# FOX's running sums of the forget gates spread to all partitions by a DMA through DRAM, in a two-layer block of four mixers on one NeuronCore

## Chip, cores and metric

One NeuronCore of a Trainium2 chip runs the whole program in one launch. The metric is the device time of one execution in microseconds (us), lower is better. All tensors are fp32. The large products split both operands into a high and a low fp32r part and add three products (high by high, high by low, low by high).

## What is computed

Two layers over 512 tokens of width 1024. Each layer has a mixer with four branches (FOX, dilated attention, retention, MLA), gates, an output projection and a feed-forward part. The change concerns FOX, a causal softmax attention with four heads of width 64 whose scores get a decay: for each head the running sum over the tokens of the log of a forget gate.

```python
log_f = jax.nn.log_sigmoid((ff + b_forget).astype(jnp.float32))
decay = jnp.cumsum(log_f, axis=1).transpose(0, 2, 1)
o_a = causal_block_attention(heads(fq, FOX_HEADS), heads(fk, FOX_HEADS), heads(fv, FOX_HEADS),
                             HEAD_DIM ** -0.5, decay)
...
s = jnp.einsum('bhqd,bhkd->bhqk', qi, k).astype(jnp.float32) * scale
s = s + args[2][..., :, None] - decay[..., None, :]
s = jnp.where(kpos[None, :] <= qpos[:, None], s, -jnp.inf)
p = jax.nn.softmax(s, axis=-1).astype(v.dtype)
return jnp.einsum('bhqk,bhkd->bhqd', p, v)
```

The decay enters twice: of the query's token (one value per partition, since queries lie on the partitions) and of the key's token (one value per column, the same in all partitions). The second is what has to be spread.

## The kernel before

**The large products and their weights.** Activations lie with features on the partitions. The projections and the gates run through `fm` (line 997 ff.): for one tile of 128 output features, 8 k-tiles of three products each, 24 weight products of 128 x 512 (`mm3`: L529, L530, L531) into a PSUM bank `acc`. Weights stream from DRAM: SP loads a block of up to 512 KB into one of three `raw` buffers (L258), ScalarE casts it to the high part `whi` (L289), VectorE subtracts for the low part `wlo` (L290). Conversions run two blocks ahead of the block in use; a `raw` buffer is free for the next load when both its conversions are done.

**The background work.** While these products run, the attention branches are slipped in between. `collect` (end of the class) counts weight products; for every 6.5 of them (`SPACING`) it calls `step()`, which first carries out what the step before deferred (`defer`, `flush`) and then advances the first generator in a queue to its next `yield`. The queue holds, in this order: MLA's preparation, MLA, dilated attention, `forget` (the running sums), FOX, retention. Here no order is written out by hand for the engines: where each instruction stands on its engine is settled when the program is built. Each engine then takes its instructions strictly in that order, SP its DMAs too.

**The running sums.** `forget` makes the log of the gates, `nl`, as 128 x 16: partition is the token within a block of 128, column 4t + h is block t of head h. `running_sum` makes the sums of the blocks before and adds two products, with the triangle `tri` (L989) and with `ones` (L990), into one PSUM bank. VectorE copies the result to `cum`, 128 x 16 (L992).

**FOX's attention** (`attention` with `kind == FOX`). There are 16 items, head h and query block i of 128 tokens; item x needs the keys of blocks 0 to i, up to 512 columns. The items are pipelined over steps: scores of x (L672, two products into a bank `b`), then the exponent of x - 1 (L681 on VectorE adds the bias and takes the row's maximum, L683 on ScalarE makes the exponential and its row sum), the normalising of x - 2 (L690 reciprocal on VectorE, L691 on GpSimd), the transposes of x - 4 (L698 on TensorE, into a bank `b`), the split of x - 5 (L708, L709), and after the last block of a head the product with the values (L752). There are four banks `b`. Before the scores are used, `make_bias` (L660, VectorE) has to make the item's bias from the mask, the query's decay (a column of `cum`) and the key's decay `dk[h]`, a tile of 128 x 512 with the same row in every partition.

`dk[h]` is made by `spread` (lines 645 to 651): four products per head, a column of `cum` repeated 128 times against the identity (L648), into a bank `b`, and a copy by ScalarE (L651). Head 0 is spread in the first step, head h + 1 after the scores of block 1 of head h, two steps ahead of its first use.

**Around it on SP.** The key tiles of FOX are rearranged by six moves of 64 partitions from SBUF to SBUF (L1099, named L1108 in the changed file) just when FOX begins; the tables of retention are loaded later by L774.

Of the kernel before, what the change touches and what calls it, by code (L numbers as in the profile page):

```python
# [9 lines left out]
F32 = mybir.dt.float32  # L10
# [197 lines left out]
class Builder:  # L208
# [425 lines left out]
    def attention(self, kind, qk, vt, out):  # L634


        nc = self.nc
        items = [(h, i) for h in range(4) for i in range(4)]
        st = {}
        dk, pts = {}, {}  # L640
        pair = {}
        mask = self.con("dil" if kind == DIL else "causal")
        cum = self.cum if kind == FOX else None

        def spread(h):
            ps = self.ps("b")
            for t in range(4):
                nc.tensor.matmul(ps[:, 128 * t:128 * t + 128], cum[:, 4 * t + h:4 * t + h + 1].to_broadcast([128, 128]),  # L648
                                 self.con("ident"), start=True, stop=True)
            dk[h] = self.a()  # L650
            self.defer(lambda: nc.scalar.copy(dk[h], ps))  # L651

        n = len(items)
        biases = {}

        def make_bias(x):
            h, i = items[x]
            L = 128 * (i + 1)
            b = self.a()
            nc.vector.scalar_tensor_tensor(b[:, :L], dk[h][:, :L], cum[:, 4 * i + h:4 * i + h + 1],  # L660
                                           mask[:, 128 * (3 - i):512], op0=ALU.subtract, op1=ALU.add)
            biases[x] = b[:, :L]
            if i == 3:
                dk.pop(h)

        def scores(x):
            h, i = items[x]
            L = 128 * (i + 1)
            qs = slice(128 * i, 128 * i + 128)
            ps = self.ps("b")  # L670
            for j, (q, k) in enumerate(qk[h]):
                nc.tensor.matmul(ps[:, :L], q[:, qs], k[:, :L], start=j == 0, stop=j == len(qk[h]) - 1)  # L672
            st[x] = ps

        def exps(x):
            i = items[x][1]
            L = 128 * (i + 1)
            ps = st.pop(x)
            A, nm, rs = self.a(), self.small(1), self.small(1)
            bias = biases.pop(x) if kind == FOX else mask[:, 128 * (3 - i):512]  # L680
            nc.vector.tensor_tensor_reduce(out=A[:, :L], in0=ps[:, :L], in1=bias, scale=-1.0, scalar=3.0e38,  # L681
                                           op0=ALU.add, op1=ALU.min, accum_out=nm)
            nc.scalar.activation(A[:, :L], A[:, :L], AF.Exp, bias=nm, scale=-1.0, accum_out=rs)  # L683
            st[x] = A, rs

        def normalise(x):
            A, rs = st[x]
            L = 128 * (items[x][1] + 1)
            rr = self.small(1)
            nc.vector.reciprocal(rr, rs)  # L690
            nc.gpsimd.tensor_scalar(A[:, :L], A[:, :L], rr, 1.0, op0=ALU.mult, op1=ALU.mult)  # L691

        def transposes(x):
            i = items[x][1]
            A = st.pop(x)[0]
            tp = self.ps("b")
            for j in range(i + 1):
                nc.tensor.transpose(tp[:, 128 * j:128 * j + 128], A[:, 128 * j:128 * j + 128], self.con("ident"))  # L698
            st[x] = tp

        def parts(x):
            h, i = items[x]
            if i == 0:
                pts[h] = (self.ptp.tile([128, 1664], F32R, tag="pth", name="pth"),
                          self.ptp.tile([128, 1664], F32R, tag="ptl", name="ptl"))
            src = st.pop(x)[:, :128 * (i + 1)].rearrange("p (j c) -> p j c", c=128)
            hi, lo = (self.pt_blocks(t, i) for t in pts[h])
            nc.scalar.copy(hi, src)  # L708
            nc.vector.tensor_sub(lo, src, hi.bitcast(F32))  # L709

        def result(h, po):
            self.pv_sum(h, po, pair)
            if h % 2 == 1:
                out[h // 2] = self.split(pair.pop(h // 2), lo_engine=nc.gpsimd)

        def at(x, f, *args):
            if 0 <= x < n:
                f(x, *args)

        if kind == FOX:  # L720
            spread(0)
            yield
            make_bias(0)
        for x in range(n + LG + 2):

            at(x - 1, exps)
            at(x - 2, normalise)
            at(x - LG - 1, parts)
            if kind == FOX:
                at(x + 1, make_bias)  # L730

            at(x, scores)
            at(x - LG, transposes)
            if 0 <= x - LG - 2 < n and items[x - LG - 2][1] == 3:
                h = items[x - LG - 2][0]
                po = self.pv(h, pts.pop(h), vt)
                self.defer(lambda h=h, po=po: result(h, po))
            if kind == FOX and x < n and items[x][1] == 1 and items[x][0] < 3:
                spread(items[x][0] + 1)
            yield  # L740
# [241 lines left out]
    def running_sum(self, nl):  # L982
        nc = self.nc
        before = self.small(16)
        nc.vector.memset(before[:, 0:4], 0.0)
        for t in range(3):
            nc.vector.tensor_add(before[:, 4 * t + 4:4 * t + 8], before[:, 4 * t:4 * t + 4], nl[:, 4 * t:4 * t + 4])
        ps = self.ps("b")
        nc.tensor.matmul(ps[:, 0:16], self.con("tri"), nl, start=True, stop=False)  # L989
        nc.tensor.matmul(ps[:, 0:16], self.con("ones"), before, start=False, stop=True)  # L990
        self.cum = self.cp.tile([128, 16], F32, tag="cum", name="cum")
        self.defer(lambda: nc.vector.tensor_copy(self.cum, ps[:, 0:16]))  # L992
        yield
        yield

# [1018 lines left out]
```

## Time and profile before

| | |
|---|---|
| median of 3 runs | 1676.44 us (1675.61 to 1676.55) |
| profiled execution, its own time | 1679.01 us |
| its span | 1677.2 us |
| TensorE clock over the span | 0.997 of full speed |
| TensorE busy (matmuls) | 1649.3 us, 98% of the span |
| VectorE / ScalarE / GpSimd busy | 1130.8 us (67%) / 851.0 us (51%) / 358.7 us (21%) |
| FOX's spread, L648 | 64 records of 275 ns at the median, 180.9 to 1043.9 us |

Times in the rows count from the span's start. PE is TensorE's products, DVE VectorE, ACT ScalarE, POOL GpSimd, SP the engine that issues most DMAs; SPq is its sequencer. The records of TensorE's products overlap, as they are pipelined, so what a product costs is read from the start of one to the start of the next and not from its length. A product of fp32 operands (not fp32r) is recorded as two passes, so the eight records of one spread are its four products. What stands in brackets behind a row is the idle time of the engine just before it, and what ended it.

### The profile page before, as it was taken

The page shows a single profiled execution, that of the slowest core. Times are in us where ns is not written, and L with a number is a line of the kernel's source. Part 1 is how long each engine was busy: PE and PEld are TensorE (multiplying, and loading weights), DVE is VectorE, ACT ScalarE, POOL GpSimd, SP SyncE. Part 2 cuts the span into 40 slices and gives each one's busy share as a digit, 9 for nine tenths or more (in the row PEclk, how much of TensorE's full clock was granted, in tenths as well). Part 3 has the DMA queues.
Part 4 walks back from the last instruction along what each step waited for, and adds up shares of the span by engine and source line. Part 5 has one row for each costly group of instructions (what it writes and reads, how often), then busy time and mean ns, then how long its engine had stood idle before and what let it go on. Part 6 is the DMA issues. An engine that isn't in the chain of part 4 may idle for free.

```text
span 1677.2 us, 26506 instructions
## 1 busy us (share of the span) xinstructions
PE 1649.3 (98%) x9746; PEld 1463.0 (87%) x9746; DVE 1130.8 (67%) x2165; ACT 851.0 (51%) x1682; POOL 358.7 (21%) x400
## 2 busy tenths in 40 slices
PE   8999999999999999999989999999999999999997
PEld 7898888788899999988878988888888989999876
DVE  6657676556469777762286576766565687777897
ACT  6666554323456555553265665533234565555665
POOL 0244333432130000000122343333321300000000
PEclk9999999999999999999999999999999999999999
DMA  5644225667735777443245452256665247775572
GB/s 205 173 107 139 82 82 175 170 169 182 213 87 144 189 186 184 95 154 99 76 148 160 108 145 76 90 175 168 173 161 178 75 137 191 186 183 153 189 234 92
DMA packets 93698, 248.88 MB, mean 148 GB/s; under 512 B 11521, under 2 KB 23041, under 8 KB 93569
## 3 DMA queue, kind: packets, MB, share of 16 engines
q1 hardware_dynamic: 72768, 205.24, 39.0%
q0 software_dynamic: 20800, 41.95, 13.6%
q8 instruction: 77, 1.26, 0.3%
q14 instruction: 53, 0.43, 0.1%
HBM read 220.93 MB, written 31.46 MB: 150 GB/s over the span
## 4 chain that ended last, share of the span: by engine, by line
PE 89%; DVE 6%; issue 2%; ACT 1%; DMA 1%; POOL 1%; DVEq 0%; SPq 0%; POOLq 0%
PE acc L529 15%; PE acc L530 15%; PE acc L531 15%; PE b L503 4%; PE b L505 4%; PE b L504 4%; PE acc L505 3%; PE acc L504 3%; PE acc L503 3%; PE b L752 2%; PE b L672 2%; PE b L698 1%; PE acc L1891 1%; PE acc L1893 1%; PE acc L1892 1%
## 5 line engine op out<-in xcount | busy, mean ns | idle before, releaser
L529 PE MATMUL acc<-a,whi 128*128 128x512 f32 (+1 forms) x1254 | 485.5, 387 | 0.0
L531 PE MATMUL acc<-a,wlo 128*128 128x512 f32 (+1 forms) x1254 | 475.2, 379 | 0.0
L530 PE MATMUL acc<-a,whi 128*128 128x512 f32 (+1 forms) x1227 | 465.3, 379 | 0.0
L289 ACT CAST whi<-raw 128x512 fp32r<-128x512 f32 (+3 forms) x398 | 214.0, 576 | 346.5 <-PE acc L530 174.7
L290 DVE TENSOR_TENSOR wlo<-raw,whi 128x512 fp32r<-128x512 f32 (+3 forms) x398 | 271.9, 713 | 133.4 <-ACT whi L289 132.7
L531 PEld LDWEIGHTS acc<-a,wlo 128*128 128x128 f32 x1254 | 236.3, 188 | 44.7
L529 PEld LDWEIGHTS acc<-a,whi 128*128 128x128 f32 x1254 | 237.1, 189 | 40.0 <-issue 1.0
L530 PEld LDWEIGHTS acc<-a,whi 128*128 128x128 f32 x1227 | 231.9, 189 | 38.9 <-issue 1.0
L405 DVE TENSOR_TENSOR wlo<-raw,whi 128x1024 fp32r<-128x1024 f32 x132 | 157.8, 1195 | 69.0 <-ACT whi L404 67.3
L404 ACT CAST whi<-raw 128x1024 fp32r<-128x1024 f32 x132 | 135.4, 1027 | 126.6 <-PE b L504 48.0
L503 PE MATMUL b<-a,whi 128*128 128x256 f32 x560 | 158.7, 283 | 0.0
L504 PE MATMUL b<-a,whi 128*128 128x256 f32 x560 | 158.5, 283 | 0.0
L505 PE MATMUL b<-a,wlo 128*128 128x256 f32 x560 | 158.5, 283 | 0.0
L1302 DVE TENSOR_TENSOR a<-acc,a 128x512 f32<-128x512 f32 x64 | 44.1, 689 | 140.0 <-PE acc L531 140.0
L503 PE MATMUL acc<-a,whi 128*128 128x256 f32 x448 | 126.8, 283 | 0.0
L504 PE MATMUL acc<-a,whi 128*128 128x256 f32 x448 | 126.8, 283 | 0.0
L505 PE MATMUL acc<-a,wlo 128*128 128x256 f32 x448 | 126.8, 283 | 0.0
L503 PEld LDWEIGHTS b<-a,whi 128*128 128x128 f32 x560 | 107.5, 192 | 0.2
L504 PEld LDWEIGHTS b<-a,whi 128*128 128x128 f32 x560 | 107.5, 192 | 0.0
L505 PEld LDWEIGHTS b<-a,wlo 128*128 128x128 f32 x560 | 107.5, 192 | 0.0
L333 POOL DMA_DIRECT2D raw<-wts x36 | 32.3, 896 | 345.8 <-DMA raw<-wts 140.6
L521 ACT CAST a<-a 128x512 fp32r<-128x512 f32 (+1 forms) x143 | 76.6, 567 | 51.8 <-DVE a L1094 10.7
(282 smaller groups left out, 3203.6 us busy)
## 6 DMA issues: line engine op xcount, KB each, us to landing
raw<-wts SPq DMA_DIRECT2D x257, 512.0 KB, 3.9
raw<-wts POOLq DMA_DIRECT2D x36, 512.0 KB, 6.9
a<-a SPq DMA_DIRECT2D x120, 128.0 KB, 2.3
sums<-wts POOLq DMA_DIRECT2D x30, 512.0 KB, 6.6
raw<-sums SPq DMA_DIRECT2D x20, 512.0 KB, 4.1
raw<-wts SPq DMA_DIRECT2D x35, 256.0 KB, 2.9
sums<-sums POOLq DMA_DIRECT2D x10, 512.0 KB, 3.7
a<-xT SPq DMA_DIRECT2D x16, 256.0 KB, 6.0
```

The source lines that it names most:

```text
L289: todo.append(lambda hi=hi, src=src, n=n: nc.scalar.copy(hi[:, :n], src))
L290: todo.append(lambda hi=hi, lo=lo, src=src, n=n: (lo_engine or nc.vector).tensor_sub(lo[:, :n], src, hi[:, :n].bitcast(F32)))
L404: self.nc.scalar.copy(hi, src)
L405: self.nc.vector.tensor_sub(lo, src, hi.bitcast(F32))
L503: mm(o, hi[:, c], x[k][0], start=first, stop=False, skip_group_check=i in (2, 3, 4, 6))
L504: mm(o, hi[:, c], x[k][1], start=False, stop=False, skip_group_check=i in (2, 3, 4, 6))
L505: mm(o, lo[:, c], x[k][0], start=False, stop=k == 3, skip_group_check=i in (2, 3, 4, 6))
L521: nc.scalar.copy(hi, src)
L529: mm(out, w[0], x[0], start=start, stop=False)
L530: mm(out, w[0], x[1], start=False, stop=False)
L531: mm(out, w[1], x[0], start=False, stop=stop)
L1302: nc.vector.tensor_mul(z, ps, self.rB)
```

## The change

The running sums are made a second time, transposed: two more products with the operands exchanged give 16 x 128, row 4t + h is block t of head h. In the step that copied `cum`, ScalarE now also copies these rows to an SBUF tile and SP writes them to a tile in DRAM, 8 KB. `spread(h)` issues one DMA on SP that reads head h's four rows of 128 and writes them to all 128 partitions. The spread's four products and ScalarE's copy are gone. One `yield` is added in the running sums and one in FOX's attention after the first spread, so FOX's scores and retention come two steps later.

```diff
         def spread(h):
-            ps = self.ps("b")
-            for t in range(4):
-                nc.tensor.matmul(ps[:, 128 * t:128 * t + 128], cum[:, 4 * t + h:4 * t + h + 1].to_broadcast([128, 128]),
-                                 self.con("ident"), start=True, stop=True)
             dk[h] = self.a()
-            self.defer(lambda: nc.scalar.copy(dk[h], ps))
+            rows = self.cum_rows.rearrange("(t h) c -> h t c", h=4)[h:h + 1]
+            nc.sync.dma_start(dk[h].rearrange("p (t c) -> p t c", t=4), rows.to_broadcast([128, 4, 128]))
...
         if kind == FOX:
             spread(0)
+            yield
             yield
             make_bias(0)
...
         self.cum = self.cp.tile([128, 16], F32, tag="cum", name="cum")
-        self.defer(lambda: nc.vector.tensor_copy(self.cum, ps[:, 0:16]))
+        rows = self.ps("b")
+        nc.tensor.matmul(rows[0:16, 0:128], nl, self.con("tri"), start=True, stop=False)
+        nc.tensor.matmul(rows[0:16, 0:128], before, self.con("ones"), start=False, stop=True)
+        self.cum_rows = self.dram.tile([16, 128], F32, tag="cum", name="cum")
+
+        def out():
+            nc.vector.tensor_copy(self.cum, ps[:, 0:16])
+            t = self.a()
+            nc.scalar.copy(t[0:16, 0:128], rows[0:16, 0:128])
+            nc.sync.dma_start(self.cum_rows, t[0:16, 0:128])
+        self.defer(out)
+        yield
         yield
         yield
```

In the changed file the lines behind `spread` have lower numbers up to the running sums (L660 becomes L657, L681 L678, L690 L687, L698 L695) and higher ones from there on (L1099 becomes L1108).

SP, where FOX begins in the first layer, with what each DMA waits for (DVE, PE, Pool, Activation: that engine; DMAHW and a number: an earlier DMA). Before, from the third last move of the keys on:

```order
L1099 DMA a<-a 64x512 [waits DMAHW7_49]
L1099 DMA a<-a 64x512 [waits DMAHW5_49,DMAHW4_49,DMAHW0_49]
L1099 DMA a<-a 64x512 [waits DMAHW7_49,DMAHW6_49,DMAHW1_49]
L258 DMA raw<-wts 128x512 [waits DMAHW2_49,DVE_49]
L258 DMA raw<-wts 128x1024 [waits DMAHW3_49,DVE_49]
L258 DMA raw<-wts 128x1024 [waits DVE_49,Activation_49]
```

And in the changed kernel:

```order
L1108 DMA a<-a 64x512 [waits DMAHW7_49]
L1108 DMA a<-a 64x512 [waits DMAHW5_49,DMAHW4_49,DMAHW0_49]
L999 DMA cum<-a 16x128 [waits DMAHW1_49,Activation_49]
L1108 DMA a<-a 64x512 [waits DMAHW7_49,DMAHW6_49,DMAHW2_49]
L258 DMA raw<-wts 128x512 [waits DMAHW3_49,DVE_49]
L648 DMA a<-cum 128x4x128 [waits DMAHW1_49]
L648 DMA a<-cum 128x4x128 [waits DVE_49]
L258 DMA raw<-wts 128x1024 [waits DVE_49]
L648 DMA a<-cum 128x4x128 [waits DMAHW4_49,PE_49,Pool_49]
L258 DMA raw<-wts 128x1024 [waits DMAHW0_49,DVE_49,Activation_49]
L648 DMA a<-cum 128x4x128 [waits DVE_49,Pool_49]
```

The write to DRAM (L999) stands between the last two moves, the first broadcast (L648) waits for it, the second for VectorE (the sum of the first exponent), the third for TensorE (the transposes of block 2), and weight loads stand between them.

VectorE at the same place, from the copy of `cum` on (`ISA` with an `a` is the exponent's sum L681, with `sm` alone its second half). Before:

```order
L992 COPY cum<-b 128x16
L764 TENSOR_TENSOR a<-b,a 64x512
L1283 TENSOR_TENSOR a<-acc,a 128x512
L290 TENSOR_TENSOR wlo<-raw,whi 128x256 x2
L1285 SCALAR_TENSOR_TENSOR a<-a 128x512
L660 SCALAR_TENSOR_TENSOR a<-a,cum,ct 128x128
L660 SCALAR_TENSOR_TENSOR a<-a,cum,ct 128x256
L681 ISA a,sm_2326<-b,a 128x128
L681 ISA sm_2326 128x1
L660 SCALAR_TENSOR_TENSOR a<-a,cum,ct 128x384
L681 ISA a,sm_2349<-b,a 128x256
```

In the changed kernel, from the weight conversion on:

```order
L290 TENSOR_TENSOR wlo<-raw,whi 128x256
L1294 SCALAR_TENSOR_TENSOR a<-a 128x512
L657 SCALAR_TENSOR_TENSOR a<-a,cum,ct 128x128
L657 SCALAR_TENSOR_TENSOR a<-a,cum,ct 128x256
L678 ISA a,sm_2340<-b,a 128x128
L678 ISA sm_2340 128x1
L657 SCALAR_TENSOR_TENSOR a<-a,cum,ct 128x384
L290 TENSOR_TENSOR wlo<-raw,whi 128x512 x2
L1292 TENSOR_TENSOR a<-acc,a 128x512
L678 ISA a,sm_2378<-b,a 128x256
```

The first bias (L657) has nothing ahead of it that is still to come from TensorE; behind it, a pair of weight conversions and the evacuation of a gate's bank (L1292) now stand between the exponents' sums of blocks 0 and 1. On TensorE 39 weight products and two spreads stood between the running sums and the scores of block 3; now 57 weight products do, and no spread.

## Rows read from the trace of the kernel before

**Rows 1.** The page: busy time of each engine, and the chain by engine.

```profile
PE 1649.3 (98%) x9746; PEld 1463.0 (87%) x9746; DVE 1130.8 (67%) x2165; ACT 851.0 (51%) x1682; POOL 358.7 (21%) x400
...
PE 89%; DVE 6%; issue 2%; ACT 1%; DMA 1%; POOL 1%; DVEq 0%; SPq 0%; POOLq 0%
```

**Rows 2.** Windows: stretch, length, busy us by engine (instructions), clock, DMA, GB/s.

```profile
190.00:196.00 6.00, 5.77 (x30) 4.60 (x28) 5.85 (x19) 3.68 (x10) 1.74 (x2) 1.00 0.10 27
```

**Rows 3.** Timeline of TensorE, first spread: start, length, engine, line, tiles, count.

```profile
180.69 0.39 PE L531 MATMUL acc<-a,wlo 128*128 128x512 f32 x1
180.91 1.05 PE L648 MATMUL b<-ct,cum 128*128 128x128 f32 x8
181.72 0.48 PE L529 MATMUL acc<-a,whi 128*128 128x512 f32 x1
182.04 0.39 PE L530 MATMUL acc<-a,whi 128*128 128x512 f32 x1
182.27 0.39 PE L531 MATMUL acc<-a,wlo 128*128 128x512 f32 x1
```

**Rows 4.** Timeline of TensorE, scores and transposes in FOX, both layers.

```profile
189.72 0.61 PE L672 MATMUL b<-a 128*128 128x512 f32 x2
...
193.06 0.30 PE L698 MATMUL b<-ct,a 128*128 128x128 f32 x1
...
195.46 0.41 PE L698 MATMUL b<-ct,a 128*128 128x128 f32 x2 [0.23 <-DVE sm L681]
...
198.12 0.49 PE L698 MATMUL b<-ct,a 128*128 128x128 f32 x3
...
1018.42 1.05 PE L648 MATMUL b<-ct,cum 128*128 128x128 f32 x8
...
1032.98 0.41 PE L698 MATMUL b<-ct,a 128*128 128x128 f32 x2 [0.23 <-DVE sm L681]
```

**Rows 5.** Timeline of TensorE, weight products around the running sums L989 and L990.

```profile
177.46 0.39 PE L531 MATMUL acc<-a,wlo 128*128 128x512 f32 x1
...
178.37 0.40 PE L530 MATMUL acc<-a,whi 128*128 128x512 f32 x1
```

**Rows 6.** Timeline of ScalarE, conversions where FOX begins.

```profile
183.17 0.71 ACT L289 CAST whi<-raw 128x256 fp32r<-128x256 f32 x2
```

**Rows 7.** Timeline of SP's issues, from the key moves on.

```profile
181.26 4.72 SPq L1099 DMA_DIRECT2D a<-a  x6
186.07 49.70 SPq L258 DMA_DIRECT2D raw<-wts  x8
```

**Rows 8.** DMA issues: tiles, queue, count, KB each, median us to landing.

```profile
a<-a SPq DMA_DIRECT2D x120, 128.0 KB, 2.3
...
vt<-vec SPq DMA_DIRECT2D x1, 41.0 KB, 1.8
```

**Rows 9.** Line 774, retention's tables (128 x 512, 256 KB), eight loads.

```profile
DMA to landing us min/median/max: 2.8/3.9/4.4
```

**Rows 10.** Line 258, the weight loads.

```profile
DMA to landing us min/median/max: 2.5/3.6/7.5
```

**Rows 11.** Timeline of VectorE in FOX, first layer.

```profile
185.83 0.73 DVE L660 SCALAR_TENSOR_TENSOR a<-a,cum,ct 128x128 f32<-128x128 f32 x2
186.49 0.28 DVE L681 CUSTOM_DVE_ANT_0 a<-b,a 128x128 f32<-128x128 f32 x1
...
186.70 0.61 DVE L660 SCALAR_TENSOR_TENSOR a<-a,cum,ct 128x384 f32<-128x384 f32 x1
190.15 0.42 DVE L681 CUSTOM_DVE_ANT_0 a<-b,a 128x256 f32<-128x256 f32 x1 [2.84 <-PE b L672]
...
192.63 1.27 DVE L290 TENSOR_TENSOR wlo<-raw,whi 128x512 fp32r<-128x512 f32 x2
...
201.43 0.35 DVE L660 SCALAR_TENSOR_TENSOR a<-a,cum,ct 128x128 f32<-128x128 f32 x1
```

**Rows 12.** Timeline of GpSimd, normalising of block 0.

```profile
191.41 0.38 POOL L691 TENSOR_SCALAR a<-a,sm 128x128 f32<-128x128 f32 x1 [6.73 <-DVE sm L690]
```

## Prediction

> **What bounds the kernel now.** The page's first part is read first: TensorE is busy 98% of the span, VectorE 67%, ScalarE 51%, and the chain that ended last lies on TensorE for 89% of its length [rows 1]. So time taken off TensorE is time won, unless it turns into a wait. The windows come next: FOX's stage in the first layer begins near 181 us, and between 190 and 196 us VectorE is busy 5.85 of 6 us beside a TensorE that is busy 5.77 [rows 2]. The reader is to see that two engines are full there. Then the timelines, engine by engine: what one spread costs TensorE, where VectorE waits, and how TensorE waits for the softmax. The second layer repeats the first: 14.55 us after the start of the first spread TensorE waits 0.23 us for the same thing [rows 3, 4].
>
> **What is removed from TensorE.** One spread is four products, recorded as eight passes. From the start of the weight product before it to the start of the second one behind it are 182.04 - 180.69 = 1.35 us; two plain intervals there are 2 x 0.23 = 0.46 (182.04 to 182.27). A spread costs 0.89 us [rows 3]. Four heads and two layers make 8 spreads, 7.1 us. All are issued on the engine that sets the end.
>
> At this point a rule can be held against the row. Row: 0.89 us for eight passes of 128 columns, 0.11 us each [rows 3]. The Trainium skill (TensorE: Matmul & The Clock Gate, section Back-to-back issue gap) gives about 81 ns for each product of 128 columns in a stream that loads weights for each; by that 8 x 8 passes would give back 5.2 us, not 7.1. The row is of these very products, so it decides.
>
> **What is added to TensorE.** Two products per layer, of 16 rows by 128 columns. The nearest row is the pair of 128 x 16 products just ahead of them: 178.37 - 177.46 = 0.91 us less 0.46 is 0.45 us [rows 5]; half a spread, also two products, is the same 0.45. Below, a shorter weight load could halve it (0.2); above, nothing shows more than 0.5. I take 0.4, because only one of the two kinds of pipeline break is new: 0.8 us for both layers. Net on TensorE: 7.1 - 0.8 = 6.3 us won, if no wait takes its place.
>
> **ScalarE** loses eight copies of a whole bank and gets two of 16 x 128; with 51% busy I cost both at nothing. If that cover were gone it would be a gain. The freed PSUM banks cost nothing either.
>
> **The new way of the sums.** I lay the new order on the old clock. ScalarE's copy stands just behind two conversions that end at 183.88 in the old order [rows 6]; an estimate for its own end is 184.2. On SP the write to DRAM stands between the fifth and the sixth move of the key tiles, which run from 181.26 to 185.98 [rows 7]. The fifth waits until the first two have landed. With half a microsecond for an issue (an estimate: six took 4.72 us with two waits among them) and 2.3 us for a landing that is 181.26 + 0.5 + 2.3 = 184.1 us [rows 7, 8], so the write starts near 184.7, after ScalarE's copy. It is 8 KB: it lands after 1.8 us (41 KB into SBUF) to 2.3 us (128 KB) [rows 8]; I take 2.0, between the two, 186.7 us. SP holds the first broadcast until that moment; the sixth move and the next weight load (186.07) go ahead of it, so SP hardly waits there. At the second broadcast SP waits longer (below), and what queues behind it are weight loads. Eight of them were spread over 49.7 us [rows 7], each waiting for a free buffer, so some microseconds cost nothing.
>
> The broadcast is 256 KB in 512 runs of 512 B. No row shows such runs. The nearest are the 256 KB tables in runs of 2 KB: 2.8 us at least, 3.9 at the median, 4.4 at most [rows 9]. Below, it can hardly beat the small loads' 1.8 [rows 8]; above, I allow the slowest weight load, 7.5 us [rows 10]. I take the tables' median, 3.9, as the size is the same: it lands at 186.7 + 3.9 = 190.6 us.
>
> **Who waits for it.** The first bias (L660, L657 in the new file) stands on VectorE ahead of everything else, so VectorE waits with it. Before it can go on it has three biases, the first exponent's sum and now also one pair of weight conversions to do: 0.73 + 0.28 + 0.61 + 1.27, some 2.8 us with their overlaps [rows 11]. In the old order VectorE sat idle for 2.84 us until 190.15, when the scores of block 3 (TensorE, 189.72) were there [rows 4, 11]: this idle time is the cover. In the new order these scores come later: between the running sums and them stand 57 weight products in place of 39 plus two spreads. 18 x 0.23 + 0.4 - 2 x 0.89 = 2.8 us, so 192.5, and VectorE would go on at 192.95. It arrives at 190.6 + 2.8 = 193.4: **0.5 us late**. The broadcast may land up to 190.1 without any effect.
>
> From there to the transposes of block 0 the old order had slack: GpSimd's normalising ended at 191.79, TensorE came at 193.06, 1.27 us later [rows 4, 12]. The new order has two more operations of 128 x 512 ahead of the reciprocal on VectorE (L1292 and L1294; some 0.7 each, an estimate from the 0.61 of a 128 x 384 bias [rows 11]), 1.4 us, and 11 weight products in place of 12 on TensorE, 0.2 us: the slack is gone and 0.3 us is missing. Together TensorE waits 0.8 us per layer at its first transposes. The 0.23 us at the second ones was there already [rows 4].
>
> The second broadcast waits on SP until the first exponent's sum has freed its tile, and lands some 5 us later, close to its first bias; I charge nothing more. The third is issued behind the transposes of block 2; in the old order its bias followed these by 201.43 - 198.12 = 3.3 us [rows 4, 11], against 3.9 for the landing: 0.6 late on VectorE, of which half may reach TensorE, 0.3 us. The fourth is issued long ahead and is hidden. So waits take 0.8 + 0.3 = 1.1 us per layer, 2.2 us in all.
>
> **The sum:** -7.1 + 0.8 + 2.2 = -4.1 us. The profiled execution (span 1677.2, its own time 1679.01) would become 1674.9, its span 1673.1. The median of the runs shown, 1676.44, lies 2.6 us under the profiled time and becomes **1672.3 us**.
>
> **Rival 1: VectorE takes over.** For: it is full from 190 to 196 us [rows 2], and its work for each block is unchanged, while the two spreads that fell among blocks 5 to 8 gave it time. Then what is removed from there is not won: in each layer only the first two spreads count, before the first wait, 2 x 2 x 0.89 = 3.6, less 0.8 added, less 2 x 0.8 for the first transposes: -1.2 us, 1675.3. Against: from 202 us on the weight products between the blocks leave VectorE room, and TensorE's waits in the old FOX stage are only 0.23 us. The case that nothing at all comes of it, 1676.4, lies with this one; the order does show that the spreads are gone.
>
> **Rival 2: the way through DRAM is slow.** One mechanism on the other side: the first broadcast lands so late that VectorE, with the weight conversions and evacuations behind it, and then TensorE stand still. With x us from issue to landing a layer loses (x - 3.4) + 0.3 at the first broadcast and half of (x - 3.3) at the third. Break-even is a loss of 3.15, x = 5.3, a landing at 192.0; slower by over 0.2% needs x above 6.4. For: weight loads took up to 7.5 us [rows 10], the broadcast reads the same 2 KB 128 times, and a weight load starts just ahead of it [rows 7]. Against: the tables never took more than 4.4 [rows 9]. With 7.5 us the loss is 4.4 per layer at the first broadcast and 2.1 at the third: 13.0 - 6.3, slower by 6.7 us, 1683.1. The Trainium skill (DMA: Bandwidth & Descriptors, section Latency and other measured facts) has a rule to this effect: access to DRAM takes 0.2 us on average and 2 us at high load; no run here separates that from the landing times.
>
> **How the numbers follow.** About 0.2%, 3.35 us, is what a measurement of this kernel can tell from no change. The forecast (waits of 1.5 us per layer or less, x up to 4.2) 0.53, rival 1 with the zero case 0.36, rival 2 0.11. Below, no wait at all gives 1676.44 - 6.3 = 1670.1, and 0.3 more if the added products cost 0.2; above, the range takes in rival 1 and the near part of rival 2, up to 1677.5. About a tenth of the cases lies above, and less below. Faster by over 0.2% is the forecast's 0.53, within 0.2% 0.36, slower 0.11.
>
> **What would show it.** Right: no products of line 648 as they were, TensorE's time between the running sums and the end of FOX shorter by about 2 us in each layer; the first broadcast issued near 186.7 and landed near 190.6; VectorE's idle time ahead of L657 ending on that DMA, at about 190.6; TensorE's first transposes waiting for GpSimd by under 1 us. Wrong: a landing beyond 192.0, waits of TensorE for VectorE or GpSimd that add up to over 3 us in a layer (rival 2, or rival 1 if no DMA ends them), or a span in which the removed 7 us show on TensorE as idle time somewhere behind FOX.

## Result and profile after

The changed kernel takes **1690.4 us** (median of 4 runs, 1688.7 to 1691.74) against 1676.49 for the kernel before in the same comparison: a ratio of 1.0081, 95% interval [1.0066, 1.0095]. Slower by 0.8% was given a chance of 0.11, and 1690.4 lies above the range. The profiled execution took 1689.87 us, its span is 1688.1, 10.9 us more than before.

The page of the changed kernel, busy time and chain, answers to [rows 1].

```profile
PE 1649.9 (98%) x9690; PEld 1460.2 (86%) x9690; DVE 1133.8 (67%) x2165; ACT 847.2 (50%) x1676; POOL 352.9 (21%) x400
...
PE 87%; DVE 6%; DMA 2%; issue 2%; ACT 2%; POOL 1%; SPq 0%; DVEq 0%; POOLq 0%; ACTq 0%
```

TensorE has 56 records fewer and is busy for as long as before, so what the spreads took has not come off its busy time; DMA's share of the chain went from 1 to 2%. The next reading is where in the program the time is lost. The weight loads of the first running sums, by line, carry the start of FOX in both layers (their first and last start); first the kernel before, then the changed one.

```profile
L989 PEld LDWEIGHTS b<-sm,ct x4: 188/188/189, 177.5 to 1015.2; 128*128 128x128 f32 x4
```

```profile
L987 PEld LDWEIGHTS b<-sm,ct x4: 187/188/189, 175.7 to 1018.4; 128*128 128x128 f32 x4
```

Up to the running sums the changed kernel is 1.8 us ahead with the same products done, before anything that the change touches: the two executions differ by that much in their first part. From there to the second layer's it needs 842.7 us in place of 837.7, from there to the end 669.7 in place of 662.0: **5.0 us lost in the first layer, 7.7 in the second**, 12.7 in all, where the spans differ by 10.9.

**FOX is close to the forecast.** SP's issues, VectorE's first bias, TensorE's first transposes, and by line the landing times of the write (L999) and of the broadcasts (L648), in the changed kernel:

```profile
179.46 3.42 SPq L1108 DMA_DIRECT2D a<-a  x5
182.98 0.53 SPq L999 DMA_DIRECT2D cum<-a  x1
183.73 0.46 SPq L1108 DMA_DIRECT2D a<-a  x1
184.28 0.54 SPq L258 DMA_DIRECT2D raw<-wts  x1
184.87 4.67 SPq L648 DMA_DIRECT2D a<-cum  x2
```

```profile
188.19 0.75 DVE L657 SCALAR_TENSOR_TENSOR a<-a,cum,ct 128x128 f32<-128x128 f32 x2 [3.87 <-DMA a<-cum]
```

```profile
194.31 0.33 PE L695 MATMUL b<-ct,a 128*128 128x128 f32 x1 [0.17 <-POOL a L688]
```

```profile
DMA to landing us min/median/max: 1.8/1.8/1.8
```

```profile
DMA to landing us min/median/max: 3.2/3.5/4.3
```

The write goes out at 182.98, the first broadcast at 184.87; VectorE waits 3.87 us for it, and TensorE pays 0.17 us at its first transposes. Nothing here loses 5 us.

**The loss is behind FOX.** The waits of TensorE from 176 to 330 us (engine, line waited at, releaser: us in total, times, longest), changed kernel:

```profile
PE b L838 <- ACT a L832: 2.5, 1, 2.5
PE b L827 <- DVE a L762: 1.0, 1, 1.0
PE b L856 <- DVE a L846: 0.7, 1, 0.7
PE b L750 <- DVE ptl L706: 0.7, 1, 0.7
PE b L695 <- POOL a L688: 0.6, 2, 0.5
```

The kernel before, same view and stretch:

```profile
PE b L858 <- DVE a L848: 1.5, 1, 1.5
PE b L698 <- DVE sm L681: 0.2, 1, 0.2
```

In the second layer they are 3.3, 1.6, 1.0, 0.9 and 0.8 us, against 0.6 and 0.2 before. L838 makes the variances of retention's normalisation (`group_norm`), from squares (ScalarE, L832) of the centred values (VectorE, L831). Retention normalises its heads in two pairs, and it is the second pair's centring that is late here. FOX's last transposes lie 64 us back. The windows show the second half of the price; stretch, length, busy us by engine, granted clock, DMA share, GB/s, changed kernel:

```profile
286.00:291.00 5.00, 5.00 (x22) 3.78 (x21) 0.00 (x0) 1.42 (x3) 0.00 (x0) 1.00 0.81 210
291.00:296.00 5.00, 2.45 (x13) 1.87 (x12) 3.09 (x5) 0.63 (x1) 2.67 (x4) 0.92 0.54 210
296.00:301.00 5.00, 5.00 (x14) 4.03 (x15) 4.24 (x4) 1.14 (x2) 4.65 (x5) 0.50 0.97 224
301.00:306.00 5.00, 4.31 (x20) 3.34 (x19) 4.38 (x14) 0.24 (x1) 0.76 (x1) 0.89 1.24 207
```

TensorE stands still for half a window, and in the next one its granted clock is 0.50, the lower of its two levels (1.2 GHz): 14 products in place of some 24. The shares missing are 0.08, 0.50 and 0.11 of 5 us, 3.45 us; from 1135 to 1150 us (0.83, 0.50, 0.98) again 3.45. **The account:** waits of 5.5 and 7.6 us in place of 1.7 and 0.8, so 10.6 us more; 6.9 of clock; 6.3 won on products, as forecast: 11.2 of the 12.7 us lost behind the running sums. The other 1.5 us are in none of these terms.

Who is late? VectorE in the changed kernel:

```profile
284.82 0.75 DVE L860 SCALAR_TENSOR_TENSOR a<-a,gnh 128x512 f32<-128x512 f32 x1
291.11 1.28 DVE L1331 SCALAR_TENSOR_TENSOR a<-a,acc 128x512 f32<-128x512 f32 x2 [5.54 <-DMA sums<-a]
292.31 1.29 DVE L290 TENSOR_TENSOR wlo<-raw,whi 128x512 fp32r<-128x512 f32 x2
293.51 0.68 DVE L831 TENSOR_TENSOR a<-a,b 128x512 f32<-128x512 f32 x1
...
297.28 4.51 DVE L542 TENSOR_TENSOR sm<-sm 128x8 f32<-128x8 f32 x1
```

GpSimd in the changed kernel:

```profile
282.13 1.38 POOL L361 DMA_DIRECT2D sums<-a  x2
291.09 1.29 POOL L362 DMA_DIRECT2D sums<-wts  x2 [7.58 <-DMA sums<-a]
...
297.63 1.66 POOL L522 TENSOR_TENSOR a<-a 128x512 fp32r<-128x512 f32 x1
298.88 2.88 POOL L1332 TENSOR_TENSOR a<-a 128x512 f32<-128x512 f32 x2
```

VectorE in the kernel before (L833 is L831, L1322 is L1331):

```profile
287.47 0.68 DVE L833 TENSOR_TENSOR a<-a,b 128x512 f32<-128x512 f32 x1
289.36 1.28 DVE L1322 SCALAR_TENSOR_TENSOR a<-a,acc 128x512 f32<-128x512 f32 x2 [1.21 <-PE acc L530]
```

The code that meets here is not FOX's. The gates multiply into the tile `z` in place, and `make_sums` starts weight sums in DRAM with a marker, a transfer of 4 bytes out of the same tile, which only serves to hold them back until `z` exists (first two lines: the gates; third: `make_sums` on GpSimd's queue, `when` is `z`; then the gates again, `ts[0]` is `z`):

```python
if d == 0 and dp % 2 == 0 and gi > 0:
    self.make_sums(3 * l + gi - 1, ("pr", "qv")[dp // 2], z)
...
dma(d[0:1, 0:1], when[0:1, 0:1])
...
t = ts[d]
nc.vector.scalar_tensor_tensor(t, t, 1.0, ps, op0=ALU.add, op1=ALU.mult)
```

The multiply (L1331) must not overwrite `z` before the marker (L361) has read it. The marker was issued at 282.13, just behind a transfer of 512 KB on the same queue (L333, 281.37), and landed with it near 291; VectorE waited 5.54 us there (6.28 in the second layer). In the kernel before the second centring stood **ahead** of this multiply, in the changed kernel it stands **behind** it: the two steps (`yield`) that the change adds move everything behind FOX in the background work by two places. The centring thus waits for a transfer that has nothing to do with it.

### The profile page after: what moved, and what is told of

Read it like the earlier page. It is cut to its first block, busy times and chain, and to the rows that moved or that the text cites. A ratio compares the mean times of both kernels' runs of the same rounds, so it can differ in the third digit from the quotient of the medians.

```text
span 1688.1 us, 26388 instructions
## 1 busy us (share of the span) xinstructions
PE 1649.9 (98%) x9690; PEld 1460.2 (86%) x9690; DVE 1133.8 (67%) x2165; ACT 847.2 (50%) x1676; POOL 352.9 (21%) x400
## 4 chain that ended last, share of the span: by engine, by line
PE 87%; DVE 6%; DMA 2%; issue 2%; ACT 2%; POOL 1%; SPq 0%; DVEq 0%; POOLq 0%; ACTq 0%
PE acc L529 15%; PE acc L530 14%; PE acc L531 14%; PE b L503 4%; PE b L505 4%; PE b L504 4%; PE acc L505 3%; PE acc L504 3%; PE acc L503 3%; PE b L750 2%; PE b L669 2%; DVE wlo L290 1%; PE acc L1900 1%; PE acc L1902 1%; PE acc L1901 1%
## 5 line engine op out<-in xcount | busy, mean ns | idle before, releaser
L290 DVE TENSOR_TENSOR wlo<-raw,whi 128x512 fp32r<-128x512 f32 (+3 forms) x398 | 278.9, 730 | 131.1 <-ACT whi L289 130.1
L333 POOL DMA_DIRECT2D raw<-wts x36 | 31.6, 876 | 346.6 <-DMA raw<-wts 120.2
L522 POOL TENSOR_TENSOR a<-a 128x512 fp32r<-128x512 f32 x40 | 56.3, 1407 | 203.1 <-ACT a L521 193.3
```

What stands on the lines that cost most here:

```text
L290: todo.append(lambda hi=hi, lo=lo, src=src, n=n: (lo_engine or nc.vector).tensor_sub(lo[:, :n], src, hi[:, :n].bitcast(F32)))
L522: (lo_engine or nc.vector).tensor_sub(lo, src, hi.bitcast(F32))
```

## Experiments

Two theories at first. **Order:** the two added steps cost the time. **Transfer:** the way through DRAM, or SP's queue, does. Ratios are to the kernel before, with 95% intervals.

### Which part of the change costs

**order_alone.** The kernel before with the two steps and no DMA:

```diff
         self.defer(lambda: nc.vector.tensor_copy(self.cum, ps[:, 0:16]))
+        yield
         yield
         yield
...
             spread(0)
+            yield
             yield
```

> The kernel before with the two added steps and nothing else: the spreads stay products on TensorE, no DMA is added. Order theory (the two steps push retention's second normalisation behind the gate multiply that waits for a transfer on GpSimd's queue): the two long waits of TensorE at the variance products and the halved clock behind them, some 12.7 us (2.5 + 3.3 of waiting, 3.5 + 3.5 of clock), appear here too: 1689 us, 1685 to 1696. Transfer theory (the way through DRAM and SP's queue make the loss): no such wait, 1676.5, within 2 us.

1693.26 us, 1.0098 [1.0083, 1.0113]. The steps alone cost more than the whole change. TensorE's waits, 176 to 330 us (lines are 3 higher):

```profile
PE b L841 <- ACT a L835: 2.5, 1, 2.5
PE b L859 <- DVE a L849: 1.7, 1, 1.7
PE b L698 <- POOL a L691: 1.1, 2, 0.7
PE b L830 <- DVE a L765: 1.0, 1, 1.0
```

The same places as in the changed kernel, with no running sums through DRAM. The clock falls there too, but by less: 0.78 and 0.88 from 296 to 306 us, 0.83 and 0.83 from 1142 to 1152, 1.7 us in each layer. Waits and clock make some 14 of the 16 us. The transfer theory falls as the cause of the loss.

**no_yields.** The changed kernel with both added `yield` lines taken out.

> The changed kernel without its two added steps: the sums go through DRAM, but retention keeps its old place. Order theory: no wait at the second variance products and full clock there; VectorE waits longer for the first broadcast, as its bias comes two steps sooner and the transfer does not: 1672 to 1680 us. Transfer theory: the transfers come no sooner and are waited for longer, so 1690 or more.

1677.7 us, 1.0004 [0.9993, 1.0014]. The loss is gone, and so is the gain. VectorE's first bias:

```profile
189.92 0.74 DVE L657 SCALAR_TENSOR_TENSOR a<-a,cum,ct 128x128 f32<-128x128 f32 x2 [4.91 <-DMA a<-cum]
```

It waits 4.91 us, and TensorE 1.4 at the transposes and 0.8 at the scores behind it; from 194 to 200 us its clock shows 0.72. So the steps do have a use: they cover the transfer.

**after_early2.** The changed kernel, with retention's normalisation two steps earlier:

```diff
-        yield
         yield
         products(*due.pop())
-        yield
         yield
         for norm in norms:
```

> The changed kernel whole, with two steps taken out between retention's products and its normalisation, so that the second centring stands ahead of the gate multiply again. Order theory: the 12.7 us at the variance products go, 1678 us (1674 to 1681). Transfer theory: 1690, within 2 us.

1683.27 us, 1.0038 [1.0023, 1.0053]: half the loss. The second layer keeps no long wait; in the first TensorE now waits 3.8 us at the next place, the spread of the factors:

```profile
297.31 3.72 DVE L844 COPY a<-sm 128x512 f32<-128x512 f32 x1
```

VectorE's copy takes 3.72 us there (0.43 in the kernel before) while GpSimd runs two adds, from 297.78 to 300.64. That is not a wait for a semaphore, and it becomes the second suspect.

**before_late2.** The kernel before, with two steps more around `products(*due.pop())`, so that the second centring stands behind the multiply.

> The kernel before, FOX untouched, with two steps added between retention's products and its normalisation, so that the second centring stands behind the gate multiply. Order theory: TensorE waits 2.5 to 3.5 us at the second variance products of each layer and its clock falls behind that: 1689 us, 1684 to 1692. Transfer theory: nothing that it names is in this kernel, 1676.5 within 2 us.

1679.97 us, 1.0012 [1.0003, 1.0022], far under the 1684 to 1692 expected. The order of the two instructions alone is not enough: here VectorE had the marker at 288.0, just as TensorE made the means that the centring needs anyway (287.86), and the multiply waited 1.6 us. The marker has to be late as well. Why it is later against the normalisation where FOX's steps are moved was not traced further.

### Is it the marker?

**after_newbuf** and **before_newbuf.** The multiply writes into a fresh tile, so that nothing waits for the marker:

```diff
-                        t = ts[d]
-                        nc.vector.scalar_tensor_tensor(t, t, 1.0, ps, op0=ALU.add, op1=ALU.mult)
+                        t = self.a()
+                        nc.vector.scalar_tensor_tensor(t, ts[d], 1.0, ps, op0=ALU.add, op1=ALU.mult)
```

> The changed kernel, with the gate multiply writing into a fresh tile in place of the one that the 4-byte marker transfer on GpSimd's queue still reads. Marker theory (VectorE stands at the gate multiply for that transfer, 5.5 and 6.3 us, with the second centring behind it): VectorE's wait for the marker goes, TensorE's 2.5 and 3.3 us at the second variance products and the halved clock behind them go: 1678 us, 1674 to 1683. If the order as such costs the time through many small waits: 1686 or more, with the waits of about 1 us at other products left. Transfer theory (the way through DRAM): 1690 within 2 us.

> The kernel before with the same fresh tile at the gate multiply. There the second centring stands ahead of the gate multiply, and TensorE waits only 1.5 and 0.6 us behind it, so the fresh tile should be worth 0 to 2 us: 1675.5 us, 1673.5 to 1678. More than 3 us won would say that the marker had cost the kernel before too, and that the run of the changed kernel with a fresh tile shows more than what the change brought.

1684.0 us, 1.0042 [1.0029, 1.0055], and 1678.16, 1.0005 [0.9996, 1.0014]. The waits at the variance products are gone in both layers and 6.4 us with them, none of which the kernel before had to give. It is one microsecond more than the marker theory's upper end: in the first layer TensorE waits 4.4 us for the factors. VectorE there:

```profile
298.76 4.61 DVE L544 SCALAR_TENSOR_TENSOR sm<-sm,sm 128x8 f32<-128x8 f32 x1
```

and GpSimd:

```profile
299.26 1.65 POOL L522 TENSOR_TENSOR a<-a 128x512 fp32r<-128x512 f32 x1
300.50 2.83 POOL L1332 TENSOR_TENSOR a<-a 128x512 f32<-128x512 f32 x2
```

An instruction on 8 columns that takes 0.17 us elsewhere ends at 303.37, when GpSimd's block ends (303.33). It is one of the chain of such small steps that makes the inverse square roots of the variances (`rsqrt`), and the factors come out of that chain. This is not new with the change: the kernel before has it too, in front of the 1.5 us that TensorE waits at L858; GpSimd's adds end there at 298.09.

```profile
294.70 3.43 DVE L542 TENSOR_TENSOR sm<-sm 128x8 f32<-128x8 f32 x1
```

**after_sums_later** and **before_sums_later.** The sums start one pair of gates later, FOX and retention untouched: `dp % 2 == 0` becomes `dp % 2 == 1`.

> The changed kernel with the weight sums of GpSimd (the 4-byte markers and the transfers behind them) started one pair of gates later, by when retention's normalisation is over; nothing in FOX or retention is touched. Marker theory: VectorE's waits of 5.5 and 6.3 us at the gate multiply no longer stand ahead of the second centring, GpSimd's adds no longer fall into VectorE's rsqrt chain, TensorE's waits at the variance products (2.5 and 3.3) and behind them (0.7 and 1.6) and the halved clock go: 1677.5 us, 1675 to 1681, with the waits of 0.7 to 1.0 us at the other products left. If the order as such is what costs: 1685 or more.

> The kernel before with the weight sums started one pair of gates later. TensorE waited there 1.5 and 0.6 us at the last products of the normalisation, with GpSimd's adds in VectorE's chain: these go, 1675 us, 1673 to 1678. The distance to the changed kernel with the same edit is then what the change costs without the marker: 0 to 5 us by the marker theory, 10 or more if the order as such is what costs.

1683.64 us, 1.0037 [1.0024, 1.0050], and 1675.19, 0.9994 [0.9985, 1.0003]. The kernel before came out as expected, the changed one missed by 2.6 us. The second layer is free of long waits, the first is not: 3.9 us at L838. No marker is near, but

```profile
289.95 5.43 DVE L290 TENSOR_TENSOR wlo<-raw,whi 128x512 fp32r<-128x512 f32 x2
295.30 0.67 DVE L831 TENSOR_TENSOR a<-a,b 128x512 f32<-128x512 f32 x1
```

two conversions that take 1.29 us above take 5.43, while GpSimd's block runs from 290.15 to 294.21. So there are two obstacles ahead of the centring, and taking one away leaves the other.

### Both obstacles

GpSimd's block here is the low part of retention's normalised output and the adds of the second gate branch. It goes to VectorE:

```diff
-            out[m] = self.split(d, lo_engine=nc.gpsimd)
+            out[m] = self.split(d)
...
-                        (nc.vector if gi == 3 else nc.gpsimd).tensor_add(merged[dd], merged[dd], t)
+                        (nc.vector if gi in (1, 3) else nc.gpsimd).tensor_add(merged[dd], merged[dd], t)
```

**after_vec_sums_later:** the changed kernel with this and the later sums.

> The changed kernel with the weight sums one pair of gates later, and GpSimd's work at this place (the low part of retention's normalised output, the adds of the second gate branch) on VectorE. Collision theory (VectorE stands either for the marker or while GpSimd's block of some 4 us runs, and the second centring stands behind that): no conversion or rsqrt step on VectorE longer than 1.5 us at this place, TensorE's 3.9 us at the variance products of the first layer gone and its clock full: 1678 us, 1675 to 1681 (VectorE has 2 us more to do ahead of the centring, of which TensorE may wait for 1). If the wait has another cause: 1683 or more, as with the later sums alone.

1675.64 us, 0.9986 [0.9976, 0.9996]: **the whole loss against the kernel before is gone**, FOX and the two steps being what they were. TensorE's waits, 176 to 330 us:

```profile
PE b L827 <- DVE a L762: 1.0, 1, 1.0
PE b L750 <- DVE ptl L706: 0.7, 1, 0.7
PE b L695 <- POOL a L688: 0.6, 2, 0.5
```

and the clock is 1.00 in all windows from 176 to 326 and from 1110 to 1160 us. The forecast gain has not come with it: the kernel before with the later sums takes 1675.19, the same within the noise. The kernel before was not run with both repairs, so what these would give it beyond the 2 us of the later sums is not known.

**after_vec:** the same, with the markers where they were.

> The changed kernel with GpSimd's work at this place on VectorE, and the markers where they were. Collision theory: the wait for the marker stays (5 us or more on VectorE, 2.5 us or more on TensorE at the variance products, in both layers), the long rsqrt steps behind it go: 1687 us, 1684 to 1691. If GpSimd's block alone were the cause: 1680 or less.

1693.08 us, 1.0092 [1.0077, 1.0107]: worse than the changed kernel, and 2 us above the upper end expected. The marker alone keeps the centring back, with VectorE's new work between it and the multiply; TensorE waits 5.2 and 5.4 us, and the small steps of the `rsqrt` chain are short again (0.17 us).

```profile
293.03 0.69 DVE L1331 SCALAR_TENSOR_TENSOR a<-a,acc 128x512 f32<-128x512 f32 x1 [5.92 <-DMA sums<-a]
```

**order_vec_sums_later:** order_alone with both repairs.

> The kernel before with the two added steps alone (spreads on TensorE), and both repairs: later sums, GpSimd's work on VectorE. Collision theory: the 16 us that the two steps alone cost shrink to the small waits of 0.7 to 1.0 us, 1682 us, 1678 to 1685, and the changed kernel with the same repairs lies 3 to 6 us under it, which is what the exchange of products for DMA is worth in this order. If the two steps cost by anything else: 1688 or more.

1681.28 us, 1.0020 [1.0011, 1.0030]. The steps alone now cost 4 us against the kernel before and not 16; against the kernel before with the later sums it is 6. TensorE's waits at the transposes (1.1 us per layer) and at the means of retention's normalisation (L830, 1.0 us per layer) are most of what is left. And this is the clean pair for the exchange itself: same order, no obstacle, products 1681.28, DMA 1675.64, so **5.6 us are won by the exchange**. Each is a median of 10 runs that scatter by 4 us; the two profiled executions, compared from the first running sums to the end, differ by 5.2. With 0.8 us more of waits for the two layers on the side of the DMA that is some 6 us of products.

### What FOX pays, and a better version

**no_yields_sums_later:** no added steps, later sums.

> The sums through DRAM without the two added steps, with the later weight sums: the old order of retention and no marker in its way, so that what is left is FOX's own cost of the way through DRAM. If that cost eats what TensorE wins (VectorE waits 4.9 us at the first bias): 1675 us, 1673.5 to 1677, as the kernel before with the later sums. If only the marker kept the gain away: 1670, 1668 to 1672.

1675.35 us, 0.9986 [0.9977, 0.9996], level with the kernel before with later sums (1675.19). In the old order FOX's wait for the first broadcast eats what TensorE wins; the marker has no part in that. TensorE waits 1.9 and 1.6 us in the two layers, and its clock falls behind that:

```profile
192.00:198.00 6.00, 5.05 (x18) 4.10 (x19) 4.64 (x17) 2.64 (x8) 1.44 (x3) 0.72 0.00 0
1028.00:1034.00 6.00, 5.19 (x19) 4.29 (x20) 4.80 (x17) 2.78 (x10) 1.45 (x3) 0.72 0.00 0
```

The shares missing are 0.28 of 6 us in each layer. Less the 0.4 us of waits that the kernel before with the later sums has, 3.1 of waits and 3.4 of clock make 6.5 us, about as much as the exchange wins.

**early_sum** and **before_early_sum.** No added steps, and the running sums one stage sooner, ahead of the attention before FOX, in the changed kernel and the one before:

```diff
-            if kind == FOX:
+            if kind == DIL:
                 self.bg.append(("forget", self.running_sum(self.forget(z))))
```

> The changed kernel without its two added steps, with the running sums (and so the write to DRAM) made one stage sooner, ahead of the attention before FOX: the first broadcast need not wait for the write, and retention keeps its old place. Order theory: 6.3 us of TensorE's work are won, waits in FOX of 0 to 1 us per layer: 1671 us, 1669 to 1674. VectorE theory (FOX's stage is bound by VectorE, and the spreads were its breathing space): waits of TensorE for the normalising of 1 us or more stay in each layer: 1674 to 1678. Transfer theory: VectorE still waits 3 us or more at the first bias, 1678 or more.

> The kernel before (spreads on TensorE) with the running sums made one stage sooner, as in the run with early sums: the same order, and only the exchange of products for DMA apart from it. Order theory and VectorE theory alike: 1676.5, within 2 us, so that the difference to the run with early sums is the exchange alone (some 5 us by the order theory, 0 to 2 by the VectorE theory).

1684.15 us, 1.0038 [1.0026, 1.0051], and 1679.93, 1.0013 [1.0005, 1.0022]. Both theories about the exchange missed, and the line of the transfer theory fits: VectorE waited 6.10 us.

```profile
192.00 0.74 DVE L657 SCALAR_TENSOR_TENSOR a<-a,cum,ct 128x128 f32<-128x128 f32 x2 [6.10 <-DMA a<-cum]
```

The sums were in DRAM long before. But the broadcast stood on SP behind the key tiles' moves and was issued at 187.82, later than in the changed kernel (184.87). In the first layer TensorE also waited 3.6 us for a VectorE copy beside GpSimd's adds, as in after_early2. Sooner sums are no gain for the kernel before either.

**early_dk0:** as early_sum, and the first broadcast is made together with the sums, into a tile of its own, which the first `spread` then takes over (the general pool has one tile less):

```diff
+            self.dk0 = self.cp.tile([128, 512], F32, tag="dk", name="dk")
+            src = self.cum_rows.rearrange("(t h) c -> h t c", h=4)[0:1]
+            nc.sync.dma_start(self.dk0.rearrange("p (t c) -> p t c", t=4), src.to_broadcast([128, 4, 128]))
```

> As the run with early sums, and the first head's broadcast is made there too, into a tile of its own (one tile less in the general pool): FOX's first bias has its sums long before it comes. If the way through DRAM, whose first broadcast stood behind the key tiles' moves on SP, is what eats the 6.3 us won on TensorE: VectorE's wait at the first bias goes and 1671 us, 1668.5 to 1674, or 4 to 8 us more where the marker transfer comes late in the first layer. If VectorE's own work binds FOX: TensorE waits 1 us or more per layer for the normalising with no transfer waited for, 1674 to 1678.

1677.77 us, 1.0001 [0.9989, 1.0013], with runs from 1673.08 to 1682.56. The wait at the first bias is gone. The runs lie as far apart as the obstacles behind FOX are high, but whether those are the reason isn't known, since one run is profiled.

**early_dk0_sums_later:** the same with later sums.

> As the run with the early first broadcast, with the weight sums started one pair of gates later as well, so that neither the first broadcast nor the marker can be waited for. Exchange worth what was forecast: 1670 us, 1668 to 1673, and 5 to 6 us under the kernel before with the later sums. VectorE theory: within 2 us of the kernel before with the later sums.

**1673.49 us, 0.9981 [0.9972, 0.9989]**: faster than both kernels, by 3.7 us against the kernel before (1677.23 in the same comparison). Half a microsecond above the range, and only 1.7 under the kernel before with later sums, where 5 to 6 were expected; the runs of these two overlap (1672.53 to 1676.86 and 1674.11 to 1677.73), so that this part of the gain is not clear of the noise. TensorE's waits from 176 to 330 us, and the same in the second layer, with 0.2 us more at the scores:

```profile
PE b L698 <- POOL a L691: 1.1, 2, 0.6
```

It waits for the normalising with no transfer near, 2.2 us in both layers; that fits rival 1, since the normalising follows VectorE's sums, but rival 1 was not tested by itself. Some 2 us of the distance stay unexplained; the sums made sooner cost the kernel before 2.9 us, which may be the same.

## Why the prediction was wrong

**What TensorE wins** was right: 7.1 - 0.8 = 6.3 us forecast, some 6 by the clean pair (5.6 by the medians or 5.2 by the traces, and 0.8 of waits). The price of a spread from [rows 3] holds. The Trainium skill (TensorE: Matmul & The Clock Gate, section Back-to-back issue gap) gives 81 ns per product; the estimate by that, 5.2 less 0.8, is 4.4 us and fits less well.

**The way through DRAM** was right, a little too dear: the write landed after 1.8 us (2.0 taken), the broadcasts after 3.5 at the median (3.9 from [rows 9]), 4.3 at most. VectorE's bias began at 188.2, where a landing at 190.6 was forecast; 1.8 us of this are the earlier start. Rival 2 needed a landing beyond 5.3 us; it did not occur.

**The waits in FOX** were right in size: 0.6 and 0.9 us at the transposes of the two layers and 0.7 and 0.8 at the products with the values (L750 behind L706), together 1.3 and 1.7 where 1.1 was forecast. That they come so near is in part luck: the forecast put 0.8 at the first transposes, which waited 0.17 in the first layer, and named no wait at the products with the values.

**Rival 1** (VectorE binds FOX) comes nearest where the added steps are missing, though there a transfer ends the first wait; 1.1 us per layer that fit it remain in the best version.

**The step that failed is the sum's own end.** "So waits take 0.8 + 0.3 = 1.1 us per layer, 2.2 us in all": only waits inside FOX were summed. The two added steps were used for what they give (57 weight products in place of 39 ahead of the scores, the cover of the transfer), and nothing was charged for what they move: all of retention, two places later among the gates. There two instructions of VectorE change places, and the one that comes first waits for a marker on GpSimd's queue; and GpSimd's block of 4 us, which already stretched VectorE's `rsqrt` chain in the kernel before, is in the way wherever the marker is not. Order_alone shows that this is the loss (16 us without any DMA), after_vec_sums_later that these two obstacles are it (1690.4 to 1675.64 with both out of the way). The forecast had 2.2 us of waits; in the changed kernel TensorE's waits grew by 10.6 us, with 6.9 of clock on top. And the steps are not free even without the obstacles: 6 us in order_vec_sums_later against the kernel before with the later sums, which is why the exchange of products for DMA, worth 5.6, ends level there. The text named the sign, "idle time somewhere behind FOX", and gave it no mechanism and no price. The order of VectorE's instructions in retention's normalisation, in the changed kernel against the one before, would have shown the exchange.

**Clock.** A second term was missing: the new waits of TensorE cost more than their length. Around the 1.5 us of the kernel before (busy 3.54 of 5 us from 296 to 301) the windows keep 1.00; behind 2.5 and 3.3 us they show 0.50, and 3.45 us are lost each time. The length of the wait alone does not give the price: 2.5 and 2.3 us at the same place in order_alone, and 1.9 and 1.6 us in FOX without the steps, each cost 1.7 us of clock.

## What to carry to other kernels

A step inserted into a chain of background work is paid by everything behind it in the chain: list what changes places on each in-order engine there, and what the instruction now in front waits for. A gain of a few microseconds on the bounding engine is worth nothing until the places where other engines have no slack have been found; here a wait of about 3 us in each layer, more than doubled by the clock, undid it. And if a repair takes away one cause and half the loss stays, look for a second cause at the same place before doubting the first.

## What was not expected of the hardware

VectorE's instructions stretch here while GpSimd runs adds or subtractions on SBUF tiles. In the changed kernel one on 8 columns takes 4.51 us (297.28 to 301.79; others of its kind 0.17), and GpSimd's three in a row end at 301.76; the copy of 0.43 us took 3.72, two conversions of 1.29 took 5.43. VectorE did not get its turn between the three, and with GpSimd's work moved away (after_vec) the same steps take 0.17 us. The Trainium skill (SBUF — State Buffer, section SBUF: two separate sides) says that the two engines share one pair of SBUF ports, which goes to one of them for a whole instruction while the other blocks; on VectorE's side this concerns instructions in a two-port mode or with two inputs in SBUF. The trace agrees, in that the stretched instruction ends with GpSimd's block (301.79 and 301.76), and adds that GpSimd keeps VectorE out from one instruction to the next. That it is the ports no run here tests by itself.

A transfer of 4 bytes on GpSimd's queue took 3.7 us at the median of its line and up to 8.7 to land in the changed kernel. The long ones, two markers in each layer, were issued just behind a transfer of 512 KB on the same queue and landed right after it: L333 went out at 281.37 and took 9.3 us, the marker went out at 282.13 and took 8.7, and VectorE was free at 291.1. The other markers, with no such transfer still under way, took 3.5 to 4.0.
